# Layer two's output projection as seven quadrant products, with weight sums formed in DRAM

## The chip, the cores and the metric

The kernel runs on one core of one Trainium2 chip. The core has a matrix engine (TensorE, PE in the profile; its loads of stationary operands are shown apart as PEld), a vector engine (VectorE, DVE), a scalar engine (ScalarE, ACT), a third elementwise engine (GpSimd, POOL) and a queue engine (SyncE, SP) that issues nearly all transfers between DRAM and the on-chip memory. Each engine runs its own instructions in program order and waits on semaphores for the others. Matmul results lie in PSUM, which the kernel uses as eight tiles of 128 x 512 float32 (three slots acc, two tr, three s). The metric is the device time of one execution in microseconds.

## What is computed

Two layers of a decoder trunk over 512 tokens of width 1024. Each layer normalises x, projects it to 3488 columns, runs four mixers of width 256 on them (latent attention, a short gated convolution, a gated token mix, block-sparse attention), gates and concatenates their outputs to y (512 x 1024), projects y with a 1024 x 1024 weight and adds x. The change touches the last line for the second layer:

```python
def hybrid_layer(x, ...):
    h = rmsnorm(x, norm_g)
    p = h @ w_in
    ...
    y = jnp.concatenate([o_a * jax.nn.silu(g_a), o_b * jax.nn.silu(g_b),
                         o_c * jax.nn.silu(g_c), o_d * jax.nn.silu(g_d)], axis=-1)
    return y @ w_out

def reference(x, ...):
    for l in range(DEPTH):
        x = x + hybrid_layer(x, ...)
    return x
```

All of it is float32. Every operand of a matmul is split into a rounded part "hi" and a remainder "lo" (`split2`: ACT writes hi, DVE writes source minus hi), and each product is the sum of three matmuls, hi·hi, hi·lo and lo·hi (`mm3`, L250).

## The kernel before

**Tiles.** Tokens are four blocks t of 128; the width of y is eight tiles of 128, kt 0 to 7. y is kept transposed: one tile yT[kt] holds 128 columns of y for all 512 tokens. Tiles 0 and 1 come from latent attention (buffer yaa in the profile), 2 and 3 from the convolution (chs), 4 and 5 from the gated mix (u), 6 and 7 from block-sparse attention (yad). `put_y` (L785) splits each into hi and lo.

**Weights.** A weight comes in units of 512 KB, 128 x 1024. `load_units` (L316) issues one load per unit into one of two raw buffers (raw_wo for this projection), in a fixed order. `split_units` (L331) splits a raw unit in two halves of 512 columns into whi and wlo, when one of six slots is free, and so frees the raw buffer. A unit of w_o holds two k tiles of one half of the columns, so a layer's projection has eight units.

**Output projection.** `part` (L1232) runs, for a half of the columns and a token block, the eight k tiles in the order YORDER = (2, 3, 0, 1, 4, 6, 5, 7), three matmuls each, into one PSUM bank o; y tile 5 is the last one to be ready. `out_chain` (L1145) adds the bank to x (buffer xr) on DVE. In layer one it goes on to the sum of squares and, through `pre_norm` (L544), to a scale that POOL computes (buffer xss), to h on DVE, and to PE's transposes hT, from which layer two's first projection (cq, weights raw_c) starts. In layer two the row goes to DRAM, and its very last block is computed in two pieces of 256 columns, so that the last addition is short.

**Order.** The order of every engine's queue is fixed when the program is built. A small planner in the file (class `Order`) advances a clock with planned costs, starts each step of a chain when its inputs are due, and writes the instruction to its engine at that point. The planned costs set only the order; on the chip semaphores decide the time. Because queues are in order, an instruction that waits holds up everything behind it on its engine, and on SP that includes transfers.

Of the kernel before, what the change touches and what calls it, by code (L numbers as in the profile page):

```python
# [38 lines left out]
YORDER, YCUT = (2, 3, 0, 1, 4, 6, 5, 7), 6  # L39
WORDER = (1, 0, 2, 3)  # L40
TAIL = ((0, 256), (256, 512))

# [154 lines left out]
def hybrid_trunk(ctx: ExitStack, tc: tile.TileContext, x, positions, norm_g, w_c, w_f, w_t, w_o, mla_q_norm_g,  # L197
# [51 lines left out]

    def mm3(ch, n, dst, sh, sl, mh, ml, first, last):  # L250
        c = cost(n)
        yield from ch.pe(c, PE.matmul, dst, sh, mh, start=first, stop=False)
        yield from ch.pe(c, PE.matmul, dst, sh, ml, start=False, stop=False)
        yield from ch.pe(c, PE.matmul, dst, sl, mh, start=False, stop=last)

# [34 lines left out]
    def add_unit(*a):  # L290
# [220 lines left out]
    for l in range(DEPTH):  # L511
# [14 lines left out]
        L.u, L.u_ev, L.b, L.b_ev = {}, {}, {}, {}  # L526
        L.mix_ev, L.mla_ev, L.QK_ev = Event(), Event(), Event()
        L.x = [None] * NT
        for n in ("ga0", "ga1", "gd0", "gd1"):
# [14 lines left out]
    def pre_norm(L, t, xx, t0, release):  # L544
# [13 lines left out]
        release(ch)  # L558
        if t == NT - 1:
            for _ in range(2):  # L560
                (t2S if L.l else sS).put(ch)

        def half(c):
            c2 = Chain(o, tps[c])
            tp = yield from trS.get(c2, f"hT{t}_{c}_{L.l}")
            for k in range(4):
                kt = c * 4 + k
                yield from c2.pe(109.0, PE.transpose, tp[:, k * P:(k + 1) * P], h[:, kt * P:(kt + 1) * P], ident)
            hput(c2)
            yield from split2(c2, hTh[:, c * 4:c * 4 + 4, t * P:(t + 1) * P],  # L570
                              hTl[:, c * 4:c * 4 + 4, t * P:(t + 1) * P], tp.rearrange("p (k n) -> p k n", k=4))
            trS.put(c2)
            o.set(L.hT[t][c], c2.t)
        for c in range(2):
            o.spawn(half(c))

    def rope(ch, x1, x2, cb, sb, nh, nd, name):
# [78 lines left out]
    def q_chain(L, t, q_ps, t0):  # L656
        ch = Chain(o, t0)
        l = L.l
        if t == 0:
            L.Q = yield from tkS.get(ch, f"Q{l}", 96)  # L660
# [371 lines left out]
    def mla_heads(L):  # L1032
# [38 lines left out]
        yield from heads(L, "a", L.Vt, prep, qk)  # L1071
        o.set(L.mla_ev, o.now)

    def moba_heads(L):
# [70 lines left out]
    def out_chain(L, half, t, a, t0, c0=0, c1=512):  # L1145
# [10 lines left out]
        elif half == 1:  # L1156
# [6 lines left out]
            o.spawn(pre_norm(layers[l + 1], t, L.x[t], ch.t, release))  # L1163


    def main():
        m = Chain(o)

        def tok(L, n, width, t, dst, us):

            for k in range(KT):
                if n == "c" and k % 4 == 0:
                    yield from m.wait(L.hT[t][k // 4])
                if t == 0 and k % 2 == 0:
                    us.append((yield from unit(m, f"{n}{k // 2}_{L.l}")))
                wh, wlo = us[k // 2]
                yield from mm3(m, width, dst, hTh[:, k, t * P:(t + 1) * P], hTl[:, k, t * P:(t + 1) * P],
                               wh[:, k % 2, :], wlo[:, k % 2, :], k == 0, k == KT - 1)
                if t == NT - 1 and k % 2 == 1:
                    done_unit(f"{n}{k // 2}_{L.l}")  # L1180
                yield o.now

        def done_unit(name):
            if units[name].slots is not eS:
                units[name].slots.put(m)

        early_put(m)
        for L in layers:
# [7 lines left out]
            us = []  # L1196
            for t in range(NT):
                a = yield from accS.get(m, f"cq{t}_{l}")
# [9 lines left out]
            for n in SEQ:  # L1208
# [10 lines left out]
                else:  # L1219
                    a = yield from accS.get(m, f"{n}_{l}")  # L1220
                    wh, wlo = yield from unit(m, f"{n}_{l}")
                    for k in range(KT):
                        yield from mm3(m, S, a, wh[:, k, :], wlo[:, k, :], hTh[:, k, :], hTl[:, k, :],
                                       k == 0, k == KT - 1)
# [3 lines left out]

            for half in range(2):
                us = {}  # L1230
# [152 lines left out]
```

## Time and profile before

| | |
|---|---|
| median of 3 runs | 509.28 us (508.9 to 509.54) |
| the profiled execution | 508.65 us |
| its span in the trace | 506.8 us |
| granted PE clock, mean | 0.996 |
| instructions in the trace | 7665, of them 2508 matmuls |
| moved by DMA | 51.57 MB, mean 102 GB/s |

The page of the profile gives busy time for each engine, the span in 40 slices, the chain of work that ended last, and the costliest groups of instructions. Other views list instructions in order of time ("the timeline"), group them by line and shape, sum busy time in chosen windows, and give for every transfer the time from its issue to its landing. A row of the timeline has the start, the duration, the engine, the line, the operation, what it writes and reads with its shape, how often it was merged, and in brackets the idle time before it with what ended that.

### The profile page before, as it was taken

The page shows a single profiled execution, that of the slowest core. Times are in us where ns is not written, and L with a number is a line of the kernel's source. Part 1 is how long each engine was busy: PE and PEld are TensorE (multiplying, and loading weights), DVE is VectorE, ACT ScalarE, POOL GpSimd, SP SyncE. Part 2 cuts the span into 40 slices and gives each one's busy share as a digit, 9 for nine tenths or more (in the row PEclk, how much of TensorE's full clock was granted, in tenths as well). Part 3 has the DMA queues.
Part 4 walks back from the last instruction along what each step waited for, and adds up shares of the span by engine and source line. Part 5 has one row for each costly group of instructions (what it writes and reads, how often), then busy time and mean ns, then how long its engine had stood idle before and what let it go on. Part 6 is the DMA issues. An engine that isn't in the chain of part 4 may idle for free.

```text
span 506.8 us, 7665 instructions
## 1 busy us (share of the span) xinstructions
PE 498.1 (98%) x2508; PEld 423.3 (84%) x2508; DVE 349.3 (69%) x917; ACT 296.5 (58%) x891; POOL 139.2 (27%) x321
## 2 busy tenths in 40 slices
PE   6999999999999999999999999999999999999997
PEld 4898888888888888888889988888888888888886
DVE  4877975468799887635576988777868887635311
ACT  5698764567687775424247894677766777432100
POOL 6867875452000000000121488513330000000000
PEclk9999999999999999999999999999999999999999
DMA  8533415112114123464443242140142121624111
GB/s 273 165 123 114 125 43 166 41 43 66 60 43 166 52 74 109 142 175 117 143 155 126 83 125 71 55 124 2 42 167 82 43 83 49 201 84 164 66 54 50
DMA packets 20618, 51.57 MB, mean 102 GB/s; under 512 B 5985, under 2 KB 7265, under 8 KB 20578
## 3 DMA queue, kind: packets, MB, share of 16 engines
q1 hardware_dynamic: 20546, 51.08, 31.1%
q8 instruction: 20, 0.33, 0.3%
q0 software_dynamic: 32, 0.00, 0.1%
q14 instruction: 20, 0.16, 0.1%
HBM read 46.87 MB, written 4.19 MB: 101 GB/s over the span
## 4 chain that ended last, share of the span: by engine, by line
PE 90%; POOL 4%; DVE 2%; DMA 2%; ACT 1%; issue 1%; POOLq 0%; DVEq 0%
PE o L184 17%; PE kv L184 10%; PE cq L184 6%; PE sq L184 5%; PE cc L184 4%; PE gb L184 4%; PE cb L184 4%; PE gd L184 4%; PE gc L184 4%; PE ch L184 4%; PE su L184 4%; PE sa L184 3%; PE ga L184 3%; PE oa L184 2%; PE od L184 2%; PE sd L184 2%
## 5 line engine op out<-in xcount | busy, mean ns | idle before, releaser
L158 DVE TENSOR_TENSOR xr<-o,xr 128x512 f32<-128x512 f32 (+1 forms) x17 | 11.2, 658 | 42.0 <-PE o L184 42.0
L184 PE MATMUL o<-whi_wo,yTl 128*128 128x512 f32 (+1 forms) x102 | 38.4, 377 | 0.0
L184 PE MATMUL o<-wlo_wo,yTh 128*128 128x512 f32 (+1 forms) x102 | 38.4, 377 | 0.0
L184 PE MATMUL o<-whi_wo,yTh 128*128 128x512 f32 (+1 forms) x102 | 38.4, 376 | 0.0
L158 ACT ACTIVATE whi_wo<-raw_wo 128x512 fp32r<-128x512 f32 x31 | 18.3, 624 | 21.7 <-PE o L184 13.6
L158 ACT ACTIVATE pa<-pa,mna 128x256 f32<-128x256 f32 (+3 forms) x44 | 23.4, 539 | 5.2 <-DVE mna L158 5.1
L184 PE MATMUL kv<-whi_kv,hTh 128*128 128x512 f32 x64 | 26.0, 406 | 0.0
L184 PE MATMUL o<-whi_wo,yD 128*128 128x512 f32 (+1 forms) x68 | 25.7, 381 | 0.0
L158 ACT ACTIVATE pd<-pd,mnd 128x256 f32<-128x256 f32 (+3 forms) x46 | 24.5, 546 | 2.0 <-DVE mnd L158 1.5
L158 ACT ACTIVATE pha<-pTa 128x512 fp32r<-128x512 f32 (+3 forms) x32 | 13.9, 434 | 20.1 <-PE pTa L184 19.9
L184 PE MATMUL kv<-whi_kv,hTl 128*128 128x512 f32 x64 | 25.1, 392 | 0.0
L184 PE MATMUL kv<-wlo_kv,hTh 128*128 128x512 f32 x64 | 24.9, 390 | 0.0
L158 ACT ACTIVATE phd<-pTd 128x512 fp32r<-128x512 f32 (+3 forms) x32 | 13.9, 435 | 18.4 <-PE pTd L184 18.3
L184 PE MATMUL cq<-whi_c,hTh 128*128 128x416 f32 x64 | 24.3, 380 | 0.0
L184 PE MATMUL cq<-whi_c,hTl 128*128 128x416 f32 x64 | 23.3, 365 | 0.0
L184 PE MATMUL cq<-wlo_c,hTh 128*128 128x416 f32 x64 | 23.0, 360 | 0.0
L158 DVE TENSOR_TENSOR wlo_wo<-raw_wo,whi_wo 128x512 fp32r<-128x512 f32 x32 | 21.0, 687 | 2.4 <-ACT whi_wo L158 2.0
L184 PEld LDWEIGHTS o<-wlo_wo,yTh 128*128 128x128 f32 x102 | 19.2, 188 | 3.6
L184 PEld LDWEIGHTS o<-whi_wo,yTh 128*128 128x128 f32 x102 | 19.2, 188 | 3.6
L184 PEld LDWEIGHTS o<-whi_wo,yTl 128*128 128x128 f32 x102 | 19.2, 188 | 3.5
L158 DVE CUSTOM_DVE_ANT_0 pa<-sa,maskb 128x512 f32<-128x512 f32 (+3 forms) x32 | 15.0, 485 | 8.7 <-PE pTa L184 4.6
L158 DVE TENSOR_TENSOR pld<-pTd,phd 128x512 fp32r<-128x512 f32 (+3 forms) x32 | 15.5, 486 | 4.9 <-ACT phd L158 4.8
(328 smaller groups left out, 1712.8 us busy)
## 6 DMA issues: line engine op xcount, KB each, us to landing
raw_wo<-in_w_o_dram SPq DMA_DIRECT2D x16, 512.0 KB, 3.9
raw_sq<-in_w_t_dram SPq DMA_DIRECT2D x8, 512.0 KB, 3.5
raw_kv<-in_w_t_dram SPq DMA_DIRECT2D x8, 512.0 KB, 3.5
raw_c<-in_w_c_dram SPq DMA_DIRECT2D x8, 416.0 KB, 4.2
raw_ga<-in_w_f_dram SPq DMA_DIRECT2D x4, 512.0 KB, 3.6
raw_su<-in_w_f_dram SPq DMA_DIRECT2D x4, 512.0 KB, 3.5
raw_gc<-in_w_f_dram SPq DMA_DIRECT2D x4, 512.0 KB, 3.6
raw_ch<-in_w_f_dram SPq DMA_DIRECT2D x4, 512.0 KB, 3.4
```

What stands on the lines that cost most here:

```text
L158: f(*a, **k)
L184: f(*a, **k)
```

## The change

Write the four quadrants of the weight as b11, b12 (the k tiles K0 = 2, 3, 0, 1; left and right columns) and b21, b22 (the k tiles K1 = 4 to 7). y has the same quadrants: tokens 0 to 255 or 256 to 511, and K0 or K1: A11, A12 for the first tokens, A21, A22 for the last. Eight quadrant products become seven:

- Weight sums t1 = b11 + b12, t3 = b12 + b22, t2 = t1 + b22 and t4 = t2 + b21.
- y sums D = A11 - A21, S = D + A22, A12 - S and A11 - S.
- Products in this order: A11·b11, D·t3, A12·b21, A22·t4, S·t2, (A11 - S)·t1, (A12 - S)·b22. PSUM banks go on accumulating across products, so that each result is added to x when it stands in a bank: z holds b11 then b21; x holds t3 then t4; y starts as minus the b11 product, which ACT copies from PSUM to PSUM, and gathers t2, t1, b22.

Each product has two token blocks, four k tiles and three matmuls of 512 columns; the second block of the last product is done in two pieces of 256 columns, in banks of its own.

**Weight sums.** `t_sums` starts when layer one's latent attention is through. It copies quadrants from DRAM to DRAM on SP (8 copies of 512 KB), and adds others to them with accumulating transfers issued on POOL (8 of 512 KB, in pieces of 1 KB). t2 needs t1's sum, t4 needs t2's. In the order that results, the copies of t1, t3 and t2 stand among layer one's weight loads on SP, the two of t4 before and between layer two's first weight loads; the accumulations of t4 stand on POOL in the middle of the first row block's scale (xss) and behind it.

**Fourteen units** instead of eight are loaded and split; the second of each pair takes a raw buffer that Q and K of the attention have left (`tkS`).

**y sums.** `put_y` puts D in the place of A21 for K0's tiles, and writes every y tile to DRAM as float32. `s_chain` reads two tiles back, does three additions of 256 columns on DVE, and splits the results into 512 and 256 columns, in the place of h (now four tiles), which nothing reads any more.

```diff
+SEVEN = (1,)
+K0, K1, KK = (2, 3, 0, 1), (4, 5, 6, 7), (0, 2, 3, 1)
+ZPROD = ("b11", "t3", "b21", "t4", "t2", "t1", "b22")
...
+    tsum = {(l, n): dr.tile([2, P, 1024], F32, name=f"{n}_{l}") for l in SEVEN for n in ("t1", "t2", "t3", "t4")}
+    ysc = {l: dr.tile([KT, P, S], F32, name=f"ysc_{l}") for l in SEVEN}
+    def quad(l, n, j):
+        return w_o[l, int(n[2]) - 1, (K0 if n[1] == "1" else K1)[2 * j] // 2]
+    def z_src(l, n, j):
+        return tsum[l, n][j] if n in ("t1", "t2", "t3", "t4") else quad(l, n, j)
+    def t_sums(l):
+        for steps in ((("t1", "b11", "b12"), ("t3", "b12", "b22")), (("t2", "t1", "b22"),), (("t4", "t2", "b21"),)):
+            for n, a, _ in steps:
+                for j in range(2):
+                    o.clk["D"] = max(o.clk["D"], o.now) + 1500.0
+                    nc.sync.dma_start(z_src(l, n, j), z_src(l, a, j))
+                    yield o.now + 4000.0
+            yield o.now + 4000.0
+            for n, _, b in steps:
+                for j in range(2):
+                    o.clk["G"] = max(o.clk["G"], o.now) + 1000.0
+                    nc.gpsimd.dma_start(z_src(l, n, j), quad(l, b, j), accum_op=ALU.add, max_dma_last_dim=1024)
+                    yield o.now + 4000.0
+            yield o.now + 8000.0
...
+        if l in SEVEN:
+            for n in ZPROD:
+                for j in range(2):
+                    add_unit(z_src(l, n, j), 2, 512, f"{n}{j}_{l}")
+            continue
...
-            if u.name in ("c2_0", "c3_0"):
+            if u.name in ("c2_0", "c3_0") or u.name[:-3] in ZPROD and u.name[-3] == "1":
...
-    hTh = big.tile([P, KT, S], F32R, name="hTh")
-    hTl = big.tile([P, KT, S], F32R, name="hTl")
...
+            if L.l:
+                yield from c2.wait(layers[L.l - 1].h_done)
+            if c not in L.h:
+                L.h[c] = [big.tile([P, 4, S], F32R, tag=f"h{x}{c}", name=f"hT{x}{c}_{L.l}") for x in "hl"]
+            yield from split2(c2, *(z[:, :, t * P:(t + 1) * P] for z in L.h[c]), tp.rearrange("p (k n) -> p k n", k=4))
...
+        if L.seven and kt in K0:
+            yield from ch.dve(V.tensor_tensor, yv[:, 256:512], yv[:, 0:256], yv[:, 256:512], op=ALU.subtract)
+        t0 = ch.t
         yield from split2(ch, *y_tiles(L, kt), yv)
         o.set(L.y[kt], ch.t)
+        if L.seven:
+            nc.sync.dma_start(ysc[L.l][kt], yv)
+            ch.t = max(ch.t, t0 + 3000.0)
+            L.left["y", kt] = ch.t
+            if kt in K1:
+                o.spawn(s_chain(L, K1.index(kt)), None, 3)
+    def s_chain(L, kk):
+        ch = Chain(o)
+        for kt in (K0[kk], K1[kk]):
+            yield from ch.wait(L.y[kt])
+            ch.t = max(ch.t, L.left["y", kt])
+        yield from ch.wait(L.hT_free)
+        w = []
+        for kt in (K0[kk], K1[kk]):
+            w.append((yield from t2S.get(ch, f"ys{kt}_{L.l}")))
+            c2 = Chain(o, ch.t)
+            dma(c2, P * 2048, w[-1], ysc[L.l][kt])
+        a, b = w
+        ch.t = max(ch.t, c2.t)
+        yield from ch.dve(V.tensor_tensor, b[:, 256:512], b[:, 256:512], a[:, 256:512], op=ALU.add)
+        yield from ch.dve(V.tensor_tensor, b[:, 0:256], b[:, 0:256], b[:, 256:512], op=ALU.subtract)
+        c2 = Chain(o, ch.t)
+        yield from ch.dve(V.tensor_tensor, a[:, 0:256], a[:, 0:256], b[:, 256:512], op=ALU.subtract)
+        yield from split2(c2, *(z[:, kk, :] for z in L.sums[0]), b)
+        t2S.put(c2)
+        for n in ("t2", "b22"):
+            o.set(L.s[n][kk], c2.t)
+        yield from split2(ch, *(z[:, kk, :] for z in L.sums[1]), a[:, 0:256])
+        t2S.put(ch)
+        o.set(L.s["t1"][kk], ch.t)
...
+        if L.l == 0:
+            for l in SEVEN:
+                if l:
+                    o.spawn(t_sums(l), None, 4)
...
+    def z_out(L, n, i, a, t0, ev, put, c0=0, c1=512):
+        ch = Chain(o, t0)
+        for t, half, op, done in {"t3": ((2 + i, 1, ALU.subtract, False),), "b21": ((i, 0, ALU.add, True),),
+                                  "t4": ((2 + i, 0, ALU.add, False),), "t2": ((2 + i, 0, ALU.subtract, True),),
+                                  "t1": ((2 + i, 1, ALU.add, True),), "u": ((i, 1, ALU.add, False),),
+                                  "b22": ((i, 1, ALU.add, True),)}[n]:
+            yield from ch.wait(L.xr[t])
+            xx = L.x[t][:, half * 512 + c0:half * 512 + c1]
+            k = dict(in0=xx, in1=a[:, c0:c1]) if op == ALU.subtract else dict(in0=a[:, c0:c1], in1=xx)
+            yield from ch.dve(V.tensor_tensor, out=xx, op=op, **k)
+            if done and (c0, c1) != (0, 512):
+                nc.sync.dma_start(out[0, t * P:(t + 1) * P, half * 512 + c0:half * 512 + c1], xx)
+            elif done:
+                if n == "t2":
+                    yield from ch.wait(L.s4[i])
+                if n in ("t1", "t2") and L.l < DEPTH - 1:
+                    junk_ = yield from trS.get(ch, f"jk{t}{half}")
+                else:
+                    junk_ = a
+                yield from row_done(L, t, half, ch.t, junk_)
+                if n in ("t1", "t2") and L.l < DEPTH - 1:
+                    trS.put(ch)
+        o.set(ev, ch.t)
+        if n == "t4":
+            o.set(L.s4[i], ch.t)
+        if put:
+            put(ch)
...
+        def seven(L):
+            l = L.l
+            L.sums = [[big.tile([P, 4, n], F32R, tag=f"h{x}{i}", name=f"sum{x}{i}_{l}") for x in "hl"]
+                      for i, n in enumerate((512, 256))]
+            o.set(L.hT_free, o.now + PELAT)
+            us = {}
+            def left(n, kk, i):
+                c = i * P
+                if n in ("t2", "b22"):
+                    z, ev = [y[:, kk, (256 if n == "t2" else 0):] for y in L.sums[0]], L.s[n][kk]
+                elif n == "t1":
+                    z, ev = [y[:, kk, :] for y in L.sums[1]], L.s[n][kk]
+                else:
+                    kt = (K0 if n in ("b11", "t3") else K1)[kk]
+                    z, ev = [y[:, (256 if n in ("t3", "t4") else 0):] for y in y_tiles(L, kt)], L.y[kt]
+                return z[0][:, c:c + P], z[1][:, c:c + P], ev
+            def prod(n, i, a, first, c0=0, c1=512):
+                for x, kk in enumerate(KK):
+                    if (n, kk // 2) not in us:
+                        us[n, kk // 2] = yield from unit(m, f"{n}{kk // 2}_{l}")
+                    wh, wlo = us[n, kk // 2]
+                    yh, yl, ev = left(n, kk, i)
+                    yield from m.wait(ev)
+                    yield from mm3(m, c1 - c0, a[:, c0:c1], yh, yl, wh[:, kk % 2, c0:c1], wlo[:, kk % 2, c0:c1],
+                                   first and x == 0, x == 3, not first)
+                    if i == 1 and c1 == 512 and x >= 2:
+                        done_unit(f"{n}{kk // 2}_{l}")
+                    yield o.now
+            def minus(i, src, dst, t0, ev):
+                ch = Chain(o, t0)
+                yield from ch.act(A.activation, dst, src, AF.Copy, scale=-1.0)
+                o.set(ev, ch.t)
+            bank, evs = {}, {}
+            home = {"b11": "z", "b21": "z", "t3": "x", "t4": "x"}
+            slot = {"z0": accS, "z1": accS, "x0": accS, "x1": sS, "y0": sS, "y1": sS}
+            for n in ZPROD:
+                for i in range(2):
+                    b = home.get(n, "y") + str(i)
+                    ev = evs[n, i] = Event()
+                    if n in ("b11", "t3"):
+                        bank[b] = yield from slot[b].get(m, f"o{b}_{l}")
+                    else:
+                        yield from m.wait(evs[{"b21": "b11", "t4": "t3", "t2": "b11", "t1": "t2", "b22": "t1"}[n], i])
+                    a = bank[b]
+                    if (l, n, i) == (DEPTH - 1, "b22", 1):
+                        ev2 = Event()
+                        yield from z_out(L, "u", i, a, m.t, ev2, sS.put)
+                        for c0, c1 in TAIL:
+                            a = yield from accS.get(m, f"ot{c0}_{l}")
+                            yield from prod(n, i, a, True, c0, c1)
+                            o.spawn(z_out(L, n, i, a, o.now + PELAT, Event(), accS.put, c0, c1))
+                        continue
+                    yield from prod(n, i, a, n in ("b11", "t3"))
+                    if n == "b11":
+                        y = bank[f"y{i}"] = yield from sS.get(m, f"oy{i}_{l}")
+                        o.spawn(minus(i, a, y, o.now + PELAT, ev))
+                    else:
+                        o.spawn(z_out(L, n, i, a, o.now + PELAT, ev,
+                                      slot[b].put if n in ("b21", "t4", "b22") else None))
+                if n == "t3" and l + 1 < DEPTH:
+                    o.spawn(load_norm_gain(layers[l + 1]))
+                    load_params(layers[l + 1])
+            o.set(L.h_done, o.now)
...
+            if L.seven:
+                yield from seven(L)
+            else:
+                o.set(L.h_done, o.now)
+            for half in range(0 if L.seven else 2):
...
```

More of the change, by code (lines that the diff above doesn't have):

```diff
@@ L248, in split2, with mm3 @@
         yield from ch.dve(V.tensor_tensor, lo, src, hi.bitcast(F32), op=ALU.subtract)
-    def mm3(ch, n, dst, sh, sl, mh, ml, first, last):
+    def mm3(ch, n, dst, sh, sl, mh, ml, first, last, go_on=False):
         c = cost(n)
-        yield from ch.pe(c, PE.matmul, dst, sh, mh, start=first, stop=False)
-        yield from ch.pe(c, PE.matmul, dst, sh, ml, start=False, stop=False)
-        yield from ch.pe(c, PE.matmul, dst, sl, mh, start=False, stop=last)
+        k = dict(skip_group_check=True) if go_on else {}
+        yield from ch.pe(c, PE.matmul, dst, sh, mh, start=first, stop=False, **k)
+        yield from ch.pe(c, PE.matmul, dst, sh, ml, start=False, stop=False, **k)
+        yield from ch.pe(c, PE.matmul, dst, sl, mh, start=False, stop=last, **k)
     def dma(ch, nbytes, dst, src):
@@ L527, in hybrid_trunk @@
         L.mix_ev, L.mla_ev, L.QK_ev = Event(), Event(), Event()
+        L.seven = l in SEVEN
+        L.hT_free, L.h_done, L.h = Event(), Event(), {}
+        L.s = {n: [Event() for _ in range(4)] for n in ("t2", "t1", "b22")}
+        L.left, L.s4 = {}, [Event(), Event()]
+        L.QK_taken = False
+        L.torder = (2, 3, 0, 1) if l and layers[l - 1].seven else (0, 1, 2, 3)
         L.x = [None] * NT
@@ L658, in q_chain @@
         l = L.l
-        if t == 0:
+        if not L.QK_taken:
+            L.QK_taken = True
             L.Q = yield from tkS.get(ch, f"Q{l}", 96)
@@ L1163, in out_chain, with row_done, release @@
             o.spawn(pre_norm(layers[l + 1], t, L.x[t], ch.t, release))
+    def row_done(L, t, half, t0, junk_):
+        l = L.l
+        cols = slice(half * 512, half * 512 + 512)
+        if l == DEPTH - 1:
+            nc.sync.dma_start(out[0, t * P:(t + 1) * P, cols], L.x[t][:, cols])
+            return
+        ch = Chain(o, t0)
+        yield from square_half(ch, layers[l + 1], t, half, junk_, L.x[t])
+        L.left[t] = L.left.get(t, 2) - 1
+        if L.left[t]:
+            return
+        nc.sync.dma_start(x1d[t * P:(t + 1) * P, :], L.x[t])
+        tend = ch.t + 4000.0
+        def release(c):
+            v4S.put(Chain(o, max(c.t, tend)))
+        o.spawn(pre_norm(layers[l + 1], t, L.x[t], ch.t, release))
+    def z_out(L, n, i, a, t0, ev, put, c0=0, c1=512):
[25 more added lines that the diff above has]
+            put(ch)
     def main():
@@ L1173, in tok @@
                     yield from m.wait(L.hT[t][k // 4])
[L1174 removed]
+                if len(us) == k // 2:
                     us.append((yield from unit(m, f"{n}{k // 2}_{L.l}")))
                 wh, wlo = us[k // 2]
[L1177 removed]
+                hh, hl = hk(L, k)
+                yield from mm3(m, width, dst, hh[:, t * P:(t + 1) * P], hl[:, t * P:(t + 1) * P],
                                wh[:, k % 2, :], wlo[:, k % 2, :], k == 0, k == KT - 1)
[L1179 removed]
+                if t == (L.torder[-1] if n == "c" else NT - 1) and k % 2 == 1:
                     done_unit(f"{n}{k // 2}_{L.l}")
@@ L1196, in main @@
             us = []
-            for t in range(NT):
+            for t in L.torder:
                 a = yield from accS.get(m, f"cq{t}_{l}")
@@ L1222, in main @@
                     for k in range(KT):
-                        yield from mm3(m, S, a, wh[:, k, :], wlo[:, k, :], hTh[:, k, :], hTl[:, k, :],
+                        yield from mm3(m, S, a, wh[:, k, :], wlo[:, k, :], *hk(L, k),
                                        k == 0, k == KT - 1)
```

10 lines of the change are left out of this document (6 added, 4 removed).

## The prediction, made before the changed kernel was run

> **What bounds the kernel now.** I read the page first: who is busy, what clock was granted, and what the chain of work that ended last is made of.
>
> ```profile
> PE 498.1 (98%) x2508; PEld 423.3 (84%) x2508; DVE 349.3 (69%) x917; ACT 296.5 (58%) x891; POOL 139.2 (27%) x321
> PE   6999999999999999999999999999999999999997
> PEclk9999999999999999999999999999999999999999
> PE 90%; POOL 4%; DVE 2%; DMA 2%; ACT 1%; issue 1%; POOLq 0%; DVEq 0%
> ```
>
> PE is busy 98% at a steady clock and is 90% of the chain, so a matmul removed is time gained, and an idle gap put into PE is time lost, one for one. The chain in order of time shows the stage that the change replaces; two PE rows of the timeline, eight matmuls apart, give the step of the narrow ones.
>
> ```profile
> 448.15 5.44 PE su L184 x24
> ...
> 456.07 3.43 PE gc L184 x15
> 459.50 43.84 PE o L184 x216
> 503.34 0.03 issue
> 503.37 0.42 DVE xr L158
> ...
> 499.09 0.28 PE L184 MATMUL o<-whi_wo,yTl 128*128 128x256 f32 x1
> ...
> 500.05 0.28 PE L184 MATMUL o<-wlo_wo,yD 128*128 128x256 f32 x1
> ```
>
> Layer two's output projection is 216 matmuls from 459.50 to 503.34 without a gap. 24 matmuls of 512 columns take 5.44 us: 0.2267 each (the rows' own durations overlap). The narrow ones step by (500.05-499.09)/8 = 0.12. The stage has 168 wide and 48 narrow: 168 x 0.2267 + 48 x 0.12 = 43.84, its row.
>
> What DVE and ACT have to spare there is in the table by stage (columns: window; its length, then PE, PEld, DVE, ACT, POOL busy; clock; DMA share; GB/s).
>
> ```profile
> 459.30:481.30 22.00, 22.00 (x98) 18.21 (x98) 8.64 (x14) 5.74 (x10) 0.00 (x0) 1.00 0.36 128
> 481.30:503.40 22.10, 22.03 (x120) 19.03 (x118) 3.82 (x7) 0.00 (x0) 0.00 (x0) 1.00 0.15 54
> ```
>
> DVE is busy 8.64 of 22.00 us and 3.82 of 22.10, ACT 5.74 and nothing. The new work must fit there.
>
> **The change, part by part.**
>
> *Matmuls.* Seven quadrant products of 2 row blocks x 4 k tiles x 3 are 168 wide matmuls where there were 192; the last block of 12 is done in two halves: 156 wide and 24 narrow. 156 x 0.2267 + 24 x 0.12 = 38.24, so 43.84 - 38.24 = **5.60 us** go. Each product takes 5.44 us: from 459.5 the third starts at 470.4, the fourth at 475.8, the fifth (t2) at 481.3, the sixth (t1) at 486.7, the seventh at 492.1.
>
> *DVE in the new stage.* Fourteen weight units are split instead of eight, nine result additions become fourteen, and y's sums bring 12 additions of 256 columns, 4 remainders of 512 and 4 of 256. I walked DVE's queue in the order that the changed program issues it, with these rows.
>
> ```profile
> 443.36 2.49 DVE L158 TENSOR_TENSOR wlo_wo<-raw_wo,whi_wo 128x512 fp32r<-128x512 f32 x4
> ...
> 456.79 1.89 DVE L158 TENSOR_TENSOR wlo_wo<-raw_wo,whi_wo 128x512 fp32r<-128x512 f32 x3
> 460.17 0.69 DVE L158 SCALAR_TENSOR_TENSOR th_gc<-th_gc,gc 128x512 f32<-128x512 f32 x1 [1.49 <-ACT th_gc L158]
> ...
> 462.55 0.69 DVE L158 TENSOR_TENSOR yTl<-u,yTh 128x512 fp32r<-128x512 f32 x1
> ...
> L158 DVE TENSOR_TENSOR pld<-pTd,phd 128x256 fp32r<-128x256 f32 x3 | 1.3, 417 | 1.2 <-ACT phd L158 1.2
> L158 ACT ACTIVATE whi_wo<-raw_wo x31: 615/622/634, 197.0 to 479.2; 128x512 fp32r<-128x512 f32 x31
> ```
>
> Back to back, 512 columns step by (2.49-0.69)/3 = 0.60. For 256 columns the nearest row is a subtraction from PSUM, 417 ns, less the same overlap of 0.08: 0.34. The old last tile of y (number 5) is done at 463.2 in both kernels. From there to the end of t2's last weight half come 18 wide and 15 narrow instructions: 18 x 0.60 + 15 x 0.34 = 15.9. One bubble is certain: ACT copies the first product's second bank to PSUM before it converts a half of b21's second unit (464.9 + 2 x 0.62 = 466.2); the six DVE instructions ahead of that half end at 465.5, so 0.7 is lost, and the run ends at 479.8. Needed: t4's last half six matmuls into the fourth product (477.2), done by about 474; t2's by 482.6, done by 479.8. Then eight wide instructions and one narrow lie ahead of and include the addition that empties t2's first bank, which t1 goes on filling: 479.8 + 5.1 = 484.9, against 486.7. That margin of 1.8 us is the narrowest. For its 22 us DVE has 9 us of weight and gate work more or less as before and 9 us new; it is nearly full, and everything behind a late input is late with it.
>
> *SP and y's way through DRAM.* SP issues in order. It stands at the load of t4's second unit until the second t3 unit is split (about 458.0, from the row at 456.79), and six reads of y of 256 KB are behind it; the write and read of tile 5 come after them.
>
> ```profile
> raw_wo<-in_w_o_dram SPq DMA_DIRECT2D x16, 512.0 KB, 3.9
> out_dram<-xr SPq DMA_DIRECT2D x7, 256.0 KB, 2.0
> ng<-in_norm_g_dram SPq DMA_DIRECT2D x2, 256.0 KB, 3.9
> ...
> GB/s 273 165 123 114 125 43 166 41 43 66 60 43 166 52 74 109 142 175 117 143 155 126 83 125 71 55 124 2 42 167 82 43 83 49 201 84 164 66 54 50
> ```
>
> The unit lands at 458 + 3.9 = 462; at the page's best slice, 273 GB/s, each pair of reads then takes 1.9 us: 463.9, 465.8, 467.7. DVE wants them at 463.2, 464.6 and about 467.5. So it loses up to 1.2 us, some of it inside the bubble. Tile 5 is written from 462.6, lands 2.0 later, and its read takes up to 3.9: 468.5, wanted at about 472. All of it stays inside the 1.8 us, but semaphore steps between ACT and DVE that I counted as nothing may use up the rest. I price the sum at **0.5 us** of idle PE: the lower bound is 0, the upper 3 (a round trip of 5.9 instead of a hidden one, less margin and bubble), and it is nearer to 0 because DVE has 1.8 us in hand at the tightest place.
>
> *Weight sums in DRAM.* Eight copies on SP and eight accumulating transfers on POOL run beside layer one. The transfers' own time no row shows. The cost of issuing one on POOL is bounded by its only DMA; what comes late is the scale of layer two's first row block, whose POOL step has an accumulation put into its middle.
>
> ```profile
> L395 POOL DMA_DIRECT2D posi<-in_positions_dram x1: 992/992/992, 2.2 to 2.2; - x1
> 243.23 0.31 POOL L158 TENSOR_SCALAR xss<-xss 128x1 f32<-128x1 f32 x1 [15.10 <-ACT o L158]
> ...
> 244.23 1.41 DVE L158 SCALAR_TENSOR_TENSOR h<-xr,xss,ng 128x512 f32<-128x512 f32 x2 [0.92 <-POOL xss L158]
> ...
> 246.19 1.03 PE L184 MATMUL hT<-ident,h 128*128 128x128 f32 x8
> ```
>
> h is ready at 245.64, PE transposes it at 246.19: 0.55 spare. The changed order has PE do three wide matmuls more first (0.68), so 1.23 hide an issue of 0.99. I take 0; if an issue costs twice that, 0.75 is lost, and with no cover at all 2.0 for both issues of t4. The other six issues, with their waits for the copies, fall where POOL idles, four of them ahead of this wait:
>
> ```profile
> POOL gq_b L158 <- DMA gq_b<-in_mla_q_g_dram: 61.6, 1, 61.6
> ```
>
> [...]
>
> *Other edits.* Four subtractions of 256 on DVE (1.4 us) and four early writes of y lie beside a PE that is at 9 in every slice but the first and the last. The first write's tile is ready at 359 and overwritten at 371, and the next two have longer:
>
> ```profile
> 358.31 0.69 DVE L158 SCALAR_TENSOR_TENSOR yaa<-yaa,th_ga 128x512 f32<-128x512 f32 x1
> ...
> 371.22 0.68 DVE L158 TENSOR_TENSOR yaa<-oa,oba 64x512 f32<-64x512 f32 x1
> ```
>
> Splitting h into four tiles changes no work. Cost 0; uncovered, 1.4.
>
> **Sum.** Against the profiled execution's 508.65 (span 506.8 and 1.85 around it): 508.65 - 5.60 + 0.5 = 503.55. The median shown is 0.63 above that execution, so **504.2 us**.
>
> **The rivals.**
>
> *DVE becomes the bound.* If y's reads land 2 to 4 us later than worked out, or the 256-column sums cost 0.6 rather than 0.34 (15 x 0.26 = 3.9 more), t4, t2 and t1 each wait: 1 to 4 us given back, 505.3 to 508. For it: DVE has almost no idle time from 460 to 480, and one queue serves splits, sums and results. Against it: the slack of 1.8, and the window after 481.3 where only 3.82 us were used.
>
> *The accumulating transfers are slow, and SP stands still.* The second half of t4's copy waits for the sum of t2's second half and stands on SP between layer two's first two weight loads.
>
> ```profile
> cg_b<-in_mla_q_norm_g_dram SPq DMA_DIRECT2D x2, 128.0 KB, 4.3
> x<-in_x_dram SPq DMA_DIRECT2D x3, 512.0 KB, 8.0
> ...
> 183.79 15.49 SPq L259 DMA_DIRECT2D raw_wo<-in_w_o_dram  x3
> ...
> 233.89 5.72 SPq L259 DMA_DIRECT2D raw_c<-in_w_c_dram  x3
> ...
> 260.36 0.43 PE L184 MATMUL cq<-whi_c,hTh 128*128 128x416 f32 x1
> ```
>
> Its accumulations are issued at about 203 (the third weight load of that stage ends its issue at 199.3, the copy goes next). The second load of layer two then comes at 203 plus two transfers; PE needs the chain of loads by 260, and three loads with their splits take some 10 us, so PE waits from 250 on: from 23 us a transfer. At 30 us each the wait is 203 + 60 - 250 = 13: 517. Slower than before begins at about 26 us. Against it: 128 KB in rows of 1 KB landed in 4.3 us, so 512 KB in such rows is at most 17, and the slowest 512 KB took 8.0. For it: nothing here shows an accumulation.
>
> *It does not do what it says, and stays even.* The matmuls go but 4.6 to 6.6 us come back as gaps, from both of the above together: 508.3 to 510.3.
>
> **How the numbers follow.** Forecast (503.3 to 505.3) 0.64; DVE bound 0.19; even 0.06; slower 0.11, most of it the transfers, the rest DVE past 6.6. Runs of this kernel differ by 0.6 us, so about 0.2% (1.0 us) can be told from no change: faster 0.83, same 0.06, slower 0.11. The range: at its low end all 5.6 from the lowest run, 508.9, which is 503.3; at its high end most of the DVE rival: 503.2 to 507.5, leaving out under 2 in 10.
>
> **What would show it.** Right: the last stage's PE run is 38 to 39.5 us from about 459.5, with 180 matmuls; 5.44 for each product; DVE nearly without idle time between 460 and 480. A wait of PE for wlo_t, for the sums or for oy's addition shows the DVE rival. [...] The prediction is wrong if the stage is shortened by less than 4 us, or if PE has gaps before 459.

## The result, and the profile after

The changed kernel takes 503.46 us (median of four executions, 503.07 to 504.06), against 509.09 us (508.6 to 509.54) for the kernel before on the same chip: a ratio of 0.9894, 95% interval 0.9879 to 0.991. That is 5.4 us less (4.6 to 6.2). The profiled execution shown below took 504.06 us, with a span of 502.4.

The page of the kernel after, with the busy time of each engine and the make-up of the chain:

```profile
PE 492.6 (98%) x2472; PEld 417.1 (83%) x2472; DVE 368.7 (73%) x958; ACT 307.2 (61%) x913; POOL 145.8 (29%) x329
...
PE 91%; POOL 3%; DVE 2%; DMA 2%; ACT 1%; issue 1%; POOLq 0%; DVEq 0%
```

PE has 36 matmuls less and is 5.5 us less busy; DVE is 19.4 us busier, ACT 10.7, and the span does not show it. The chain in order of time, of the kernel after (start, length, what):

```profile
460.48 5.44 PE oz L187 x24
465.92 5.44 PE ox L187 x24
471.36 5.44 PE oz L187 x24
476.80 5.44 PE ox L187 x24
482.24 13.60 PE oy L187 x60
495.84 2.88 PE ot L187 x24
498.73 0.02 issue
498.75 0.42 DVE xr L161
```

Seven products stand end to end, and the stage lasts 498.73 - 460.48 = 38.25 us where it lasted 43.84. There is no gap in it. The stage begins 0.98 us later than in the profiled execution before; that shift is there, nearly whole, from the start-up on (the first reading of positions landed in 6.8 us instead of 5.0) and belongs to the execution: other executions of the changed kernel had spans of 501.3 to 501.9, and in the profiled execution with four additions below, where that reading took 5.1 us, the stage begins at 459.69.

Busy time by window, of the kernel after (the same two windows and columns as before):

```profile
459.30:481.30 22.00, 22.00 (x99) 18.22 (x98) 19.74 (x40) 14.00 (x27) 0.00 (x0) 1.00 0.80 269
481.30:502.40 21.10, 17.41 (x89) 14.71 (x87) 10.62 (x19) 2.31 (x4) 0.00 (x0) 0.98 0.31 106
```

DVE went from 8.64 to 19.74 of 22 us: nearly full, and yet always ahead of PE. How far ahead is read from its timeline in the kernel after:

```profile
465.62 0.76 DVE L161 TENSOR_TENSOR ys<-ys,ys 128x256 f32<-128x256 f32 x2 [0.21 <-DMA ys<-ysc]
...
467.11 0.69 DVE L161 TENSOR_TENSOR wlo_b<-raw_b,whi_b 128x512 fp32r<-128x512 f32 x1 [0.39 <-ACT whi_b L161]
...
480.09 0.68 DVE L161 TENSOR_TENSOR wlo_t<-raw_t,whi_t 128x512 fp32r<-128x512 f32 x1
...
485.23 0.68 DVE L161 TENSOR_TENSOR xr<-xr,oy 128x512 f32<-128x512 f32 x1
```

Only one of the reads of y made DVE wait at this place, for 0.21 us, and one wait for ACT cost 0.39. t2's last half is split at 480.77. The addition that empties y's first bank ends at 485.91. In the chain t1, which fills that bank again, begins at 482.24 + 5.44 = 487.68, 1.77 us later. The chain counts a product from the end of the matmul before it, though; t1's first matmul itself starts at 487.52 in PE's timeline, so 1.61 us are in hand, less the time that PE takes to start after the bank is free.

### The profile page after: what moved, and what is told of

Same layout as the page of the kernel before. It is cut to its first block, busy times and chain, and to the rows that moved or that the text cites. A ratio compares the mean times of both kernels' runs of the same rounds, so it can differ in the third digit from the quotient of the medians.

```text
span 502.4 us, 7746 instructions
## 1 busy us (share of the span) xinstructions
PE 492.6 (98%) x2472; PEld 417.1 (83%) x2472; DVE 368.7 (73%) x958; ACT 307.2 (61%) x913; POOL 145.8 (29%) x329
## 3 DMA queue, kind: packets, MB, share of 16 engines
q0 software_dynamic: 4256, 4.20, 5.8%
## 4 chain that ended last, share of the span: by engine, by line
PE 91%; POOL 3%; DVE 2%; DMA 2%; ACT 1%; issue 1%; POOLq 0%; DVEq 0%
PE kv L187 10%; PE o L187 9%; PE cq L187 6%; PE sq L187 5%; PE cc L187 4%; PE gb L187 4%; PE cb L187 4%; PE gd L187 4%; PE ch L187 4%; PE su L187 4%; PE gc L187 4%; PE sa L187 3%; PE ga L187 3%; PE oy L187 3%; PE ox L187 2%; PE oz L187 2%
## 5 line engine op out<-in xcount | busy, mean ns | idle before, releaser
L328 POOL DMA_DIRECT2D t<-in_w_o_dram x8 | 8.8, 1153 | 37.3 <-DMA t<-t 37.2
L161 ACT ACTIVATE hTh<-hT 128x512 fp32r<-128x512 f32 x16 | 9.3, 597 | 16.7 <-PE hT L187 16.6
L187 PE MATMUL sq<-yTh,hTh 128*128 128x512 f32 x48 | 18.9, 393 | 0.0
L187 PE MATMUL o<-whi_wo,yTh 128*128 128x512 f32 x48 | 18.8, 391 | 0.0
L187 PE MATMUL sq<-yTh,hTl 128*128 128x512 f32 x48 | 18.7, 390 | 0.0
L187 PE MATMUL sq<-yTl,hTh 128*128 128x512 f32 x48 | 18.7, 390 | 0.0
L187 PE MATMUL o<-whi_wo,yTl 128*128 128x512 f32 x48 | 18.7, 389 | 0.0
L187 PE MATMUL o<-wlo_wo,yTh 128*128 128x512 f32 x48 | 18.7, 389 | 0.0
L161 DVE TENSOR_TENSOR pla<-pTa,pha 128x512 fp32r<-128x512 f32 (+3 forms) x32 | 15.4, 484 | 4.1 <-ACT pha L161 3.9
L161 DVE CUSTOM_DVE_ANT_0 pd<-sd,maskb 128x256 f32<-128x256 f32 (+3 forms) x32 | 15.1, 484 | 1.0 <-PE pTd L187 0.8
```

The source lines that it names most:

```text
L161: f(*a, **k)
L187: f(*a, **k)
L328: nc.gpsimd.dma_start(z_src(l, n, j), quad(l, b, j), accum_op=ALU.add, max_dma_last_dim=1024)
```

## The experiments

Where a loss or gain in us against the changed kernel is given below, it is the difference of the two ratios to the kernel before, times 509.1. A ratio is known to about 0.0015, or 0.8 us, and so a difference of two to about 1 us.

### The matmuls, and the sums alone

With `SEVEN` empty the kernel has the old projection again; h stays in four tiles.

```diff
-SEVEN = (1,)
+SEVEN = ()
```

> The changed file with the seven products, the weight sums and y's way through DRAM all left out for the second layer, so that only h in four tiles and the rewritten bookkeeping remain; the output projection is the old one of eight units. Theory (the whole gain is the 24 matmuls that go, 5.60 us, and nothing else of the edit moves the time): 509.1 us, within 0.5 of the kernel before. Rival (part of the gain comes from h's four tiles or from another order of the queues): clearly below 509, down to 506.

Measured: 509.08 us, ratio 1.0 (0.9991 to 1.001). In the second kernel the projection is the old one too, but the weight sums are formed all the same, and nothing reads them.

```diff
-SEVEN = (1,)
+SEVEN = ()
+TS = (1,)
...
-            for l in SEVEN:
+            for l in TS:
                 if l:
                     o.spawn(t_sums(l), None, 4)
```

> The old projection in both layers, with the copies and accumulating transfers of the weight sums issued all the same and their results left unread: 8 MB more of DRAM traffic beside layer one and POOL's eight issues. Theory (all of it lies beside a PE that never waits for it): 509.1 us, no idle PE between 130 and 270. Rival (contention with the weight loads or POOL's issues cost something that the changed kernel hides in its gain): 510 to 512.

Measured: 508.76 us, 0.9989 (0.9979 to 0.9998). The eight copies and eight accumulating transfers, 8.4 MB more moved beside layer one (59.5 against 51.1), cost nothing that can be measured. So the whole gain comes from the shorter stage.

### The accumulating transfers and their issue on POOL

How such a transfer looks, in the kernel after: first the page's rows of issues (KB each, median us to landing), then the timeline where t4's two stand in the middle of layer two's first scale and behind it.

```profile
t<-in_w_o_dram POOLq DMA_DIRECT2D x8, 512.0 KB, 8.1
...
raw_t<-t SPq DMA_DIRECT2D x8, 512.0 KB, 3.6
```

```profile
244.55 1.09 POOL L328 DMA_DIRECT2D t<-in_w_o_dram  x1
245.28 0.99 POOL L161 TENSOR_TENSOR xss<-xss,nhalf 128x1 f32<-128x1 f32 x1
245.82 1.50 POOL L328 DMA_DIRECT2D t<-in_w_o_dram  x1
...
246.30 1.41 DVE L161 SCALAR_TENSOR_TENSOR h<-xr,xss,ng 128x512 f32<-128x512 f32 x2 [2.04 <-POOL xss L161]
...
247.81 1.03 PE L187 MATMUL hT<-ident,h 128*128 128x128 f32 x8
```

512 KB land in 8.1 us (median of eight; 9.6 at most), over twice the 3.6 of a plain load, and far from the 23 us at which the prediction saw harm. h is ready at 247.71, 0.10 before PE's first transpose. Two kernels make this dearer. One cuts each transfer into pieces a quarter as long:

```diff
-...accum_op=ALU.add, max_dma_last_dim=1024)
+...accum_op=ALU.add, max_dma_last_dim=256)
```

> The changed kernel with its accumulating transfers cut into pieces of 256 bytes instead of 1 KB, four times as many. Theory (a transfer's landing and its issue on POOL go by the number of pieces, and the second copy of t4 stands on SP behind t2's sums): landing up to 32 us instead of 8.1 and issue up to 4.2 us instead of 1.05; the second half of t2's sum then lands about 205 + 2 x 32 less the overlap, 255 to 265, and PE, which can cover until about 250, waits 5 to 15 us: 509 to 519; from the issue alone 3 us (h of the first row block has 0.1 us in hand): 506.5 at the least. Rival (cost goes by bytes, not pieces): landing 8, issue 1.0, 503.5 us.

Measured: 503.66 us, 0.9893 (0.9878 to 0.9908). The packets of POOL's queue, in the page of this kernel:

```profile
q0 software_dynamic: 16544, 4.20, 9.7%
```

There were 4256 before the cut. An issue on POOL then takes 1.85 us instead of 1.05 (medians), and a transfer lands in 10.1 instead of 8.1. Four times the pieces made the issue 1.8 times as long and the landing 1.25 times, so the expectation that the price goes by the number of pieces, and with it 506.5 us at the least, fell; the rival, that it goes by bytes alone, is nearer. The other kernel issues a second transfer behind each, into a spare tensor that nothing reads:

```diff
                     nc.gpsimd.dma_start(z_src(l, n, j), quad(l, b, j), accum_op=ALU.add, max_dma_last_dim=1024)
+                    nc.gpsimd.dma_start(scr[j], quad(l, b, j), accum_op=ALU.add, max_dma_last_dim=1024)
```

> Each of the eight accumulating transfers is followed on POOL by one more of the same size into a spare DRAM tensor. Theory: the transfers themselves (4.2 MB more, 8 us each) cost nothing; the issue put into POOL's scale of layer two's first row block makes h another 1.05 us later, and PE pays what is beyond the cover that is left, 0.4 to 0.9 us: 503.9 to 504.6. Rival 1: SP or the memory is the limit and the copies behind the longer sums hold up layer two's first weight loads: above 506. Rival 2: h has more cover than the 0.1 us read from its row: 503.5.

Measured: 503.99 us, 0.9901 (0.9887 to 0.9914). The time alone cannot tell 0.3 us from nothing; the timeline of this kernel can:

```profile
246.80 0.39 PE L187 MATMUL o<-whi_wo,yD 128*128 128x512 f32 x1
247.39 1.38 PE L187 MATMUL hT<-ident,h 128*128 128x128 f32 x8 [0.20 <-DVE h L161]
248.52 0.48 PE L187 MATMUL o<-whi_wo,yTh 128*128 128x512 f32 x1
```

The transposes start 0.59 after the matmul before them instead of 0.23, and take 1.13 to the next matmul instead of 0.79: 0.70 us lost. POOL's step is 1.04 us longer there (3.14 from the start of its first instruction to the end of its second, against 2.10), so 0.34 was covered. In the kernel with short pieces the same reading gives a step 0.80 longer, 0.45 lost, 0.35 covered. Both agree: the cover is 0.35 us. It is more than the 0.10 read from the row. The row merges two halves of h, and the second half is needed four transposes later than the first; that fits, but was not tried by itself.

### How much DVE has in hand

Additions of 256 columns into a scratch tile that nothing reads, 4, 8, 14 or 20 of them, are put on DVE ahead of the addition that takes b21's first bank (here fourteen):

```diff
+        if n == "b21" and i == 0:
+            for _ in range(14):
+                V.tensor_tensor(junk, maskb[:, 0:256], maskb[:, 256:512], op=ALU.add)
```

> The changed kernel with four extra additions of 256 columns on DVE (0.34 us each, 1.4 us in all) ahead of the addition of the first b21 bank, writing to a scratch tile that nothing reads there. Theory (DVE has 1.8 us in hand at its tightest place, the addition that empties y's first bank before t1): PE does not wait, 503.5 us as the changed kernel. Rival (DVE is the bound already, or has no margin): 504.8.

> As the run with four, but fourteen extra additions, 4.8 us. Theory: 4.8 less the margin of 1.8 is 3.0 us of idle PE in the last stage, first for t2's second unit and then for y's first bank: 506.5 us. Rival (the idle time of DVE in the window after 481, about half of it, takes the delay up): 503.5. Rival (each us on DVE counts in full): 508.2.

> Eight additional DVE instructions at the same place as the fourteen. Theory: with fourteen (6.39 us) PE stood 3.3 us in t2, so DVE is 3.1 us ahead of t2 there; eight of them are 3.65 us, PE waits about 0.6 us, too short to lower the granted clock: 503.9 to 504.4. Rival: the narrowest margin is 1.8 us and a wait always brings the low clock with it: 505.3 to 507.

> Twenty additional DVE instructions, 9.1 us, at the same place. Theory: 9.1 - 3.1 = 6.0 us of waiting in t2 and one stretch of about 3.3 us at half clock after it, 1.6 us: 511.1. Rival: the low clock costs in proportion to the wait (1.5 us for 3.3, so 2.8 for 6.0): 512.4. Rival: without any such cost 509.5.

| additions | DVE time added | median, ratio (95%) | lost | added minus lost |
|---|---|---|---|---|
| 4 | 1.8 us | 503.79, 0.9897 (0.9883 to 0.9912) | 0.2 | 1.6 |
| 8 | 3.7 | 505.72, 0.9935 (0.9922 to 0.9949) | 2.1 | 1.6 |
| 14 | 6.4 | 508.48, 0.9994 (0.9984 to 1.0005) | 5.1 | 1.3 |
| 20 | 9.2 | 511.73, 1.0047 (1.0035 to 1.006) | 7.8 | 1.4 |

(The time added is the step between two of them, (6.39 - 0.42)/13 = 0.459, times their number.) The loss grows one for one with what is added, beyond 1.3 to 1.6 us. An addition cost 0.46 us here and not the 0.34 that the expectations of four and fourteen took, so fourteen were 6.4 us and not 4.8; that is why they came out at 508.5 and not at 506.5. With four, the loss is too small for the times alone, but the chain of that kernel shows it:

```profile
481.45 5.44 PE oy L187 x24
486.97 8.45 PE oy L187 x36
```

DVE has emptied the bank at 486.83 in its timeline, and PE starts t1 0.14 later, at 486.97; going by the step of the matmuls before, it would have started at 486.73. So PE did wait, 0.24 us, against the expectation, and 1.84 - 0.24 = 1.6 us were covered.

My first reading of the fourteen was another: PE stood 3.3 us in t2, so I took DVE to be 3.1 us ahead there and expected eight to cost 0.6. That fell. What the eight show, in that kernel's timeline:

```profile
484.15 0.50 PE L187 MATMUL oy<-wlo_t,sumh 128*128 128x512 f32 x1 [1.29 <-DVE wlo_t L161]
485.36 0.50 PE L187 MATMUL oy<-wlo_t,sumh 128*128 128x512 f32 x1 [0.24 <-DVE wlo_t L161]
...
489.76 0.69 DVE L161 TENSOR_TENSOR xr<-xr,oy 128x512 f32<-128x512 f32 x1
...
490.60 0.47 PE L187 MATMUL oy<-whi_t,sumh 128*128 128x512 f32 x1 [1.05 <-DVE xr L161]
```

PE waits twice in t2 and once more for the bank that t1 fills: DVE has emptied it at 490.45, and 0.15 later PE starts t1. (This was the longest of the five executions; its reads of y landed later too.) With fourteen, the bank is emptied at 491.41 and t1 starts at 491.69, right behind the matmul before it: PE does not wait for the bank there, because it came as late in another way. The timeline of the kernel with fourteen, and below it its windows:

```profile
485.12 0.50 PE L187 MATMUL oy<-wlo_t,sumh 128*128 128x512 f32 x1 [1.51 <-DVE wlo_t L161]
...
487.34 0.63 PE L187 MATMUL oy<-whi_t,sumh 128*128 128x512 f32 x1
487.77 0.63 PE L187 MATMUL oy<-wlo_t,sumh 128*128 128x512 f32 x1
```

```profile
485.00:486.00 1.00, 0.88 (x3) 0.49 (x3) 1.00 (x3) 0.95 (x2) 0.00 (x0) 0.94 0.97 262
486.00:487.00 1.00, 0.82 (x3) 0.58 (x3) 1.00 (x3) 0.00 (x0) 0.00 (x0) 0.50 0.91 348
487.00:488.00 1.00, 1.00 (x4) 0.81 (x3) 1.00 (x3) 0.46 (x1) 0.00 (x0) 0.50 1.03 180
488.00:489.00 1.00, 1.00 (x3) 0.76 (x3) 1.00 (x4) 0.69 (x2) 0.00 (x0) 0.50 0.92 348
```

After the waits in t2 the granted clock is 0.50 for over three microseconds, and matmuls step by 0.43 instead of 0.227. Waits of 3.3 us and 1.8 us of slow matmuls make the 5.1. At full clock PE would have come 1.8 us earlier and waited for the bank, which it could have used from about 491.41 + 0.15 = 491.56 on. So with four and eight the emptying of y's first bank, in DVE's queue, sets when t1 starts; with fourteen it is within 0.13 us of doing so, whatever PE's waits in t2 look like. With twenty the bank was empty at 494.56 and t1 started at 495.20: there the slow matmuls ended last, by half a microsecond, and the expectation, 511.1, came close because two errors offset: it had 6.0 us of waits and 1.6 of low clock, the trace has some 5.6 and 2.5.

### Both layers by seven products

Here the aim was a faster kernel: the same for layer one takes another 24 wide matmuls away, 24 x 0.2267 = 5.44 us.

```diff
-SEVEN = (1,)
+SEVEN = (0, 1)
...
+        o.spawn(t_sums(0), 60000.0, 4)
```

> The changed kernel with the seven products in both layers; the first layer's weight sums are started at a planned 60 us. Theory (a matmul removed is time gained, and all that is added finds cover): another 5.6 us go, 497.9 us; up to 2 us of it come back because the first layer's stage also has squares on ACT, the next layer's weights on ACT and DVE, and POOL's scales behind the accumulations: 497.9 to 500. Rival (the first layer's stage is too full, or POOL, which then waits for copies in the middle of the rotary steps, holds up the heads): 503 or more.

Measured: 512.94 us, 1.0073 (1.0056 to 1.009), slower than before. PE's waits in this kernel (total, times, longest):

```profile
PE pTd L187 <- DVE kl1d L161: 3.8, 1, 3.8
...
PE oy L187 <- ACT whi_t L161: 2.5, 1, 2.5
PE hT L187 <- DVE hTl L161: 2.5, 1, 2.5
```

The first lies in the second attention of layer one. Its cause, in the timeline of the same kernel:

```profile
177.86 0.42 SPq L849 DMA_DIRECT2D ysc<-chs  x1
...
184.45 0.59 ACT L161 ACTIVATE mk1d<-tmkd 64x512 fp32r<-64x512 f32 x1 [5.03 <-DMA ysc<-chs]
```

A write of y stood on SP behind a weight load, was issued at 177.86 and landed after 6.5 us; ACT waited 5.03 us for the buffer. I took the sums' traffic for the cause of all three and moved it: layer one's sums to 15 us, layer two's to 320 us.

```diff
-        o.spawn(t_sums(0), 60000.0, 4)
+        o.spawn(t_sums(0), 15000.0, 4)
+        o.spawn(t_sums(1), 320000.0, 4)
```

> Both layers by seven products, with layer one's sums started at 15 us instead of 60 and layer two's at 320 us instead of the middle of layer one. Theory: the run with both layers lost 5.5 us in layer one's rotary and second attention stage because a write of y landed in 6.5 us beside the sums' traffic and held a buffer that ACT needed; without that traffic there the loss goes, and part of what PE waited in layer one's output projection: 505 to 508. Rival: DVE, full from start to end of that projection, and not the traffic, sets the time there and the order of the queues sets it in the rotary stage: 511 to 513.

Measured: 513.53 us, 1.0084 (1.0069 to 1.0099). The wait in the attention is gone, and another in the projection has grown. Its timeline:

```profile
232.32 0.85 SPq L264 DMA_DIRECT2D raw_t<-t  x2
233.23 0.42 SPq L525 DMA_DIRECT2D cg_b<-in_mla_q_norm_g_dram  x1
...
240.93 0.95 SPq L264 DMA_DIRECT2D ng<-in_norm_g_dram  x2
241.98 0.38 SPq L264 DMA_DIRECT2D raw_t<-t  x1
...
251.99 0.80 PE L187 MATMUL oy<-whi_t,sumh 128*128 128x512 f32 x1 [5.62 <-DVE xr L161]
```

Neither theory had this. SP issues layer two's thirteen parameter loads (the expectation below says fourteen) and two of its norm gain between the loads of t1's two units, so the second unit is loaded nearly 9 us late. The row names DVE's addition xr, which empties the bank for t1; the chain of this kernel leads from it back to the unit:

```profile
241.98 5.67 DMA raw_t<-t
...
248.39 0.59 DVE wlo_t L161
...
251.33 0.61 DVE xr L161
```

The addition stands in DVE's queue behind the splits of the late unit. PE stands 5.6 us. The granted clock is 0.77 over the window from 245 to 260, but for part of its low time PE had nothing to do: t1's first 24 matmuls take 7.29 us instead of 5.44, so the low clock costs 1.85 us and not the 3.4 of the expectation below. Now nine of the thirteen go to SP in the middle of layer one, the four others behind t1:

```diff
-                    load_params(layers[l + 1])
+                if n == "t1" and l + 1 < DEPTH:
+                    load_rest(layers[l + 1])
...
+                    if n == "gd1" and not l:
+                        load_params(layers[1])
```

> As the run with both layers and their sums apart, but nine of layer two's parameter loads go to SP in the middle of layer one and the five others after t1, instead of all fourteen between the loads of t1's two weight units. Theory: SP issues in order, so t1's second unit was issued some 8 us late and PE stood 5.6 us and then ran at half clock for some 7 us (3.4 us lost); with the unit early, both go: 504.5, between 502.5 and 507. Rival: DVE's work in that stage is the limit, and t1 is late all the same: 510 or more.

Measured: 508.03 us over 12 executions that range from 505.68 to 511.47, 0.9989 (0.9967 to 1.001). The wait of 5.6 is gone. That brought 4.8 us where 9 were expected, or 7.5 with the low clock at 1.85; the rest of the difference stays open. A part of what is left shows in the timeline of this kernel, some 15 us apart:

```profile
58.70 1.10 POOL L328 DMA_DIRECT2D t<-in_w_o_dram  x1
59.45 1.95 POOL L161 TENSOR_TENSOR mmq<-mmq,nhalf 128x4 f32<-128x4 f32 x1
...
73.41 0.38 PE L187 MATMUL mp<-vnh,wsh 128*128 128x256 f32 x1 [2.15 <-ACT vnh L161]
```

An accumulating transfer is issued into POOL's queue where POOL has been on the chain that PE waits for from 58.70 to 69.30. The last kernel holds layer one's accumulating transfers back until 72 us:

```diff
-            yield o.now + 4000.0
+            yield max(o.now + 4000.0, 0.0 if l else 72000.0)
```

> As the run before, but layer one's accumulating transfers are not issued before 72 us. Theory: in that run two of them, 1.1 us each, stood in POOL's full queue near 59 us and PE waited 2.8 us for POOL's chain behind them, with low clock after it, about 4 us in all: 504.0, between 502.5 and 506. Rival: PE's wait there comes from ACT and DVE, whose order also changed, and the sums' later traffic costs again in the rotary stage: 508 or more.

Measured: **501.6 us** (500.87 to 502.34), ratio 0.9854 (0.9837 to 0.9871): faster than both, 2.0 us less than the changed kernel. Its chain:

```profile
215.10 5.44 PE oz L187 x24
...
231.42 5.44 PE ox L187 x24
236.86 10.89 PE oy L187 x48
...
478.95 13.60 PE oy L187 x60
```

Both projections run without a gap. Of the 5.44 us that layer one's projection gives, 2.0 were gained and about 3.4 are still lost (to about 1 us): 1.5 where PE, done with layer one's projection, waits for a split of h on DVE (hTl) before it goes on with layer two's transposes, 0.6 where it waits for vnh in layer two; the rest was not found. Two gaps of PE in layer one's projection (1.1 and 0.6 us in the kernel before this one) also went, which the edit did not aim at; they are most of the 2.4 us by which it came out below its expectation. The whole order of the queues shifts with each such edit, and I did not separate that.

## Why the prediction was right

Forecast 504.2 us, measured 503.46.

- **Matmuls, 5.60 us.** 43.84 - 38.25 = 5.59. The kernel with the old projection returned to 509.08, so nothing else paid.
- **Stall, 0.5 us: mis-sized.** It was 0. DVE waited 0.21 us for a read of y and 0.39 for ACT where 1.2 and 0.7 had been allowed, and both stayed inside the margin. Together with the comparison runs of the kernel before, 0.19 below the median that the sum started from, this makes up most of the 0.74 us between forecast and result.
- **DVE's walk.** t2's last half forecast at 479.8; 480.77 less the shift of 0.98 is 479.8. The narrowest place forecast as the emptying of y's first bank, with 1.8 us; the trace has 1.77 counted the same way, from the chain, and 1.61 to the start of t1's first matmul. Less the hand-over from DVE to PE, which was left out (0.14 and 0.15 in the runs with four and eight additions), that is about 1.5, and adding work there showed 1.3 to 1.6. The 256-column price, 0.34, is the step from 471.13 to 471.46 to 471.80 in DVE's rows.
- **y's last tile.** This term was mis-sized. The write was forecast to land in 2.0 us and its read in up to 3.9. SP issued the write at 463.56, stood 5.1 us for it, and could issue the read only at 469.62; the read then landed in 2.6 us, at 472.2. That is 8.7 us for the way instead of 5.9. DVE did not wait, since it comes to that read only at 473.0, 0.8 later. This was luck of the place: with both layers, a slow write of y, landing in 6.5 us, did stop ACT for 5.03 us.
- **Issue on POOL, 0 us.** Forecast 0.99 us with 0.24 to spare; measured 1.05, and 0.35 to spare. The forecast that a doubled issue would cost 0.75 is borne out by the 0.70 of the run with doubled transfers. The eight issues took 1.0 to 1.5 us each.
- **The slow rival** wanted 23 us a transfer; 8.1 was measured, and 10.1 in short pieces. POOL did wait 37.2 us in all for copies that were behind SP's weight loads, but nothing that PE needed stood behind those waits.
- **The DVE rival** was real, 1.5 us away. The runs with additions price it: past that, one for one.

## What to carry to other kernels

Trading matmuls for elementwise work paid here by the whole matmul time, 5.59 us, because DVE, which does the work, kept ahead at its tightest place, by 1.3 to 1.6 us; find that place by walking the queue in issue order, and test it by adding known work there, at more than one size. When the same trade was moved to layer one, the matmul times carried over (5.44 us a product there too, in the last run) but the queues didn't: what stood between two weight loads on SP, or behind a DMA issue on POOL, cost more than the trade gained (512.94, 513.53 and 508.03 us against 503.46), and changing the order alone brought part of it back (501.6). A wait that is seen first, or that is longest, need not be the one that sets the end.

## What the runs showed of the hardware

Some waits of PE had a second price. In the run with fourteen additions, waits of 3.3 us within five were followed by some 3.4 us at a granted clock of 0.50. With both layers, a pause of 2.6 us (last matmul before it issued at 248.26, next at 251.13), one matmul and a pause of 0.5 more were followed by matmuls 0.43 apart from 252.6 to 255.6 (clock 0.56 over 252 to 254 and 0.59 over 254 to 256, so some 3.4 us at 0.50). With both layers and the sums apart, in the wait of 5.6 us, the clock fell some 2.6 us after PE had run out of work (last matmul issued at 245.98; clock 1.00 over 246 to 248, 0.72 over 248 to 250, which makes the fall at about 248.9, then 0.50). There, and with twenty additions, the low clock lasted about 6.7 us (248.9 to 255.6; 486.4 to 493.1). With eight additions, where PE waited 1.9 us in t2 and, after nearly four microseconds of work, 1.2 more, the clock stayed at 1.00. So the slow stretches were some 3.4 us long in two of the runs and about 6.7 in two others; what length of wait brings one on, and what ends it, these runs don't show.

An accumulating transfer from DRAM to DRAM of 512 KB landed in 8.1 us against 4.6 to 4.8 for a plain copy; cut into four times as many packets it landed in 10.1, and its issue on POOL went from 1.05 to 1.85 us.
